# Layer 0's norm factor moved behind the projections: x transposed as it comes, norm weights applied as it leaves PSUM

## The chip, the cores and the metric

One core of a Trainium2 chip runs the whole program. The metric is the device time in microseconds of one execution. TensorE (PE) multiplies and transposes, VectorE (DVE), ScalarE (ACT) and GpSimd (POOL) work elementwise, SyncE (SP) issues most transfers. GpSimd has no part of PSUM in this kernel; VectorE and ScalarE empty it.

## What is computed

A two-layer encoder over 1024 tokens of width 1024. Layer 0 mixes by a neighbourhood attention with 16 heads, layer 1 by a grouped-query attention. The part that matters here is the head of layer 0:

```python
def rms_norm(x, g):
    xf = x.astype(jnp.float32)
    y = xf * lax.rsqrt(jnp.mean(xf * xf, axis=-1, keepdims=True) + NORM_EPS)
    return (y * g.astype(jnp.float32)).astype(x.dtype)

h = rms_norm(x, norm_g[0])
q, k, v, gate = jnp.split(h @ w_in, 4, axis=-1)     # w_in: 1024 x 4096
# attention of each query over an 8 x 16 window of the 16 x 64 grid, with a bias
x = x + (attention * silu(gate)) @ w_out
g = sigmoid(rms_norm(x, ple_norm_g[0]) @ ple_w_gate[0])
x = x + g * (p[0] @ ple_w_proj[0])
```

The norm factor of a token, r = rsqrt(mean(x^2) + eps), is one number per token; the norm weight norm_g[0] is one number per channel. A projection sums over channels, so r can be multiplied in after it.

## The kernel before

Tokens are kept in 8 tiles of 128. All products are made in float32r from a high and a low part: an operand is rounded (ScalarE writes the high part), the rest is found by subtraction (VectorE writes the low part), and three products high x high, high x low, low x high are summed in PSUM (`split3`, line 301 in the profile). The transposed input of the projections lies in `HTh` and `HTl` (channel on the partition, 8 token tiles x 8 channel blocks).

The program order is written out by hand: each engine runs its instructions in the order in which the Python code emits them. Two helpers shape that order. The class `Weights` (`WQ`) stages weight units of 128 x 1024 over SP's queue into `wstage`, and `pump` splits one into `wh` (ScalarE, line 216) and `wl` (VectorE, line 217; `settle` emits that half, at the next pump unless asked for earlier). `post` holds pieces of work that are emitted some steps later.

The opening of `mixer_a` (lines 695 to 780) makes the values V of heads 0 to 3 while x arrives. For each token tile: `square(t)` sums x^2 on ScalarE into `stat`; `newton(a, b)` finds r by small VectorE operations (lines 313 to 323, 714); `scale(t)` multiplies x by r and by the norm weights, which were broadcast to all partitions (`gain`, a transfer of 512 KB): for tiles 0, 1, 2, 4 and 6 in one VectorE operation (line 726), for 3, 5 and 7 on ScalarE (line 728) and then POOL (line 729). `ht(t)` transposes the eight 128 x 128 blocks on TensorE (line 426), rounds them out of PSUM (line 427) and subtracts (line 428). `vs[t][0]` and `vs[t][1]` are the two halves of the V projection of a tile, 12 products each; its eviction writes V's high part (ScalarE, line 580) and low part (VectorE, line 581). `weave` interleaves the Newton steps with other work. Transfers go out in the order x tile 0, gain, x tile 1, two weight units, x tiles 2 to 7, then the mask, the bias table and its rearrangement (`U`, `U2`).

After the opening, q and k of head 0 are projected (the first of those products has the form `d<-HTh,wh` of 128 x 512 on line 301), and then come 16 heads of attention, with the q/k projection of the next head, the gate projection and V of the next four heads as filling between the steps (`mix`). One step, for a head and a query tile: products S (`f_S`), bias and row minimum on VectorE (line 650, `sp` and `mn`), exponentials on ScalarE (line 659), transposes on TensorE (line 667), high and low parts `PTh` (ScalarE, line 670) and `PTl` (VectorE, line 671), products with V (`f_AV`). The eviction of a q/k projection (`qk_evac`) copies PSUM to `raw` (tile `th`) on ScalarE (line 594), then writes `QS`, `KA`, `KB` in three later pieces: two roundings on ScalarE (lines 597, 598), two differences and two copies on VectorE (601, 602, 603, 606). The eviction of a gate projection copies PSUM to `G` on ScalarE (line 521) and takes the tanh (line 522).

## Time and profile before

| what | us |
|---|---|
| three timed executions | 1574.35, 1575.03, 1576.03 |
| their median | 1575.03 |
| profiled execution, its time | 1577.5 |
| profiled execution, span from first to last instruction | 1575.6 |
| TensorE busy in the span | 1523.6 |
| VectorE busy | 1023.9 |
| ScalarE busy | 871.4 |
| POOL busy | 269.5 |

Busy times add up what each engine's instructions took; matmuls overlap, so TensorE's is not work at its peak. Around the span lie 1.9 us that no instruction shows. The mean granted TensorE clock is 0.997.

### The profile page before, as it was taken

The numbers are of one execution on the slowest core, as the hardware profiler recorded it, in microseconds if no ns is written. First come the engines' busy times: TensorE is split into PE (matmuls) and PEld (weight loads), VectorE is DVE, ScalarE is ACT, GpSimd is POOL, SyncE is SP. The second block draws the span as 40 slices with busy tenths as digits, with TensorE's granted clock in tenths as the row PEclk, the third lists the DMA queues.
The fourth block names the chain that finished last, engine by engine and source line by source line (L and its number), as shares of the span: only waits on it lengthen the run. The fifth ranks groups of instructions, "written<-read, shape, count | busy, mean of one in ns | idle before, by whom it ended". The sixth has DMA issues, their size and how long they took to land.

```text
span 1575.6 us, 24284 instructions
## 1 busy us (share of the span) xinstructions
PE 1523.6 (97%) x9048; PEld 1328.7 (84%) x9048; DVE 1023.9 (65%) x2062; ACT 871.4 (55%) x1744; POOL 269.5 (17%) x372
## 2 busy tenths in 40 slices
PE   6999999999999999999999999999999999999997
PEld 5888988988988788888988889989899888778886
DVE  6566576376467435648877786777777877525636
ACT  6465465366366622433467676766667767622422
POOL 2102102112022010000222132443131200000023
PEclk9999999999999999999999999999999999999999
DMA  8212122132122972142210111102111213651213
GB/s 272 78 45 65 53 80 78 39 92 78 39 79 77 343 257 68 54 140 94 74 49 21 38 51 41 58 24 65 39 32 43 74 41 112 223 201 54 71 55 129
DMA packets 89861, 138.84 MB, mean 88 GB/s; under 512 B 16912, under 2 KB 55952, under 8 KB 89744
## 3 DMA queue, kind: packets, MB, share of 16 engines
q1 hardware_dynamic: 85136, 122.62, 23.8%
q10 hardware_dynamic: 4608, 14.68, 2.6%
q8 instruction: 71, 1.16, 0.3%
q14 instruction: 46, 0.38, 0.1%
HBM read 104.65 MB, written 36.15 MB: 89 GB/s over the span
## 4 chain that ended last, share of the span: by engine, by line
PE 41%; DVE 7%; ACT 3%; issue 2%; ACTq 0%; DVEq 0%
PE d L301 21%; PE o L301 8%; PE t L1070 5%; PE s L301 5%; DVE PTl L1073 2%; DVE mn L1054 1%; ACT PTh L1072 1%; DVE wl L217 1%; PE t L426 1%; ACT wh L216 1%; PE t L1024 0%; ACT P L1060 0%; DVE QS L1034 0%; DVE ss L901 0%; DVE KB L965 0%
## 5 line engine op out<-in xcount | busy, mean ns | idle before, releaser
L301 PE MATMUL d<-wh,HTh 128*128 128x256 f32 (+1 forms) x1096 | 372.3, 340 | 5.0 <-ACT HTh L427 2.3
L301 PE MATMUL d<-wh,HTl 128*128 128x256 f32 (+1 forms) x1096 | 365.8, 334 | 1.5 <-DVE HTl L428 1.5
L301 PE MATMUL d<-wl,HTh 128*128 128x256 f32 (+1 forms) x1096 | 365.2, 333 | 0.0
L1073 DVE TENSOR_TENSOR PTl<-t,PTh 128x512 fp32r<-128x512 f32 x256 | 164.4, 683 | 114.8 <-ACT PTh L1072 114.4
L301 PEld LDWEIGHTS d<-wh,HTh 128*128 128x128 f32 x1096 | 207.7, 189 | 28.3 <-ACT HTh L427 2.9
L301 PEld LDWEIGHTS d<-wh,HTl 128*128 128x128 f32 x1096 | 207.7, 189 | 24.1 <-DVE HTl L428 2.2
L301 PEld LDWEIGHTS d<-wl,HTh 128*128 128x128 f32 x1096 | 208.0, 190 | 21.6
L301 PE MATMUL d<-HTh,wh 128*128 128x512 f32 x504 | 205.9, 409 | 0.0
L301 PE MATMUL d<-HTh,wl 128*128 128x512 f32 x504 | 197.8, 392 | 0.0
L301 PE MATMUL d<-HTl,wh 128*128 128x512 f32 x504 | 197.5, 392 | 0.0
L1060 ACT ACTIVATE P<-s,mn 128x1024 f32<-128x1024 f32 x128 | 142.7, 1114 | 66.6 <-DVE mn L1054 65.7
L301 PE MATMUL o<-PTl,V 128*128 128x256 f32 (+2 forms) x672 | 175.6, 292 | 3.3 <-DVE PTl L1073 2.2
L301 PE MATMUL o<-PTh,V 128*128 128x256 f32 (+2 forms) x672 | 174.2, 289 | 2.6 <-ACT P L1060 1.1
L1072 ACT ACTIVATE PTh<-t 128x512 fp32r<-128x512 f32 x256 | 139.4, 592 | 44.9 <-PE t L1070 44.3
L1054 DVE TENSOR_REDUCE mn<-s 128x1 f32<-128x1024 f32 x128 | 154.7, 1209 | 10.9 <-PE s L301 10.8
L1070 PE MATMUL t<-ident,P 128*128 128x128 f32 x1024 | 136.9, 275 | 7.6 <-DVE PTl L1073 6.1
L217 DVE TENSOR_TENSOR wl<-wstage,wh 128x1024 fp32r<-128x1024 f32 x89 | 113.8, 1284 | 40.8 <-ACT wh L216 40.3
L301 PEld LDWEIGHTS o<-PTl,V 128*128 128x128 f32 x672 | 128.9, 192 | 10.7 <-DVE PTl L1073 6.5
L301 PEld LDWEIGHTS o<-PTh,V 128*128 128x128 f32 x672 | 128.7, 192 | 8.3 <-issue 1.5
L1070 PEld LDWEIGHTS t<-ident,P 128*128 128x128 f32 x1024 | 115.0, 140 | 22.2 <-DVE PTl L1073 15.6
L301 PE MATMUL s<-KA,QS 128*128 128x512 f32 (+2 forms) x384 | 133.6, 402 | 0.0
L301 PE MATMUL s<-KB,QS 128*128 128x512 f32 (+2 forms) x384 | 121.8, 371 | 0.0
(178 smaller groups left out, 2436.9 us busy)
## 6 DMA issues: line engine op xcount, KB each, us to landing
wstage<-in_wts SPq DMA_DIRECT2D x92, 512.0 KB
X<-in_x SPq DMA_DIRECT2D x16, 512.0 KB
pp<-ppD SPq DMA_DIRECT2D x32, 256.0 KB
rb<-rD SPq DMA_DIRECT2D x56, 128.0 KB
ppD<-th SPq DMA_DIRECT2D x24, 256.0 KB
xD<-X SPq DMA_DIRECT2D x8, 512.0 KB
X<-xD SPq DMA_DIRECT2D x8, 512.0 KB
yD0h<-rb SPq DMA_DIRECT2D x14, 256.0 KB
```

What stands on the lines that cost most here:

```text
L216: act.activation(hi, s, AF.Copy)
L217: self.rest = lambda: dve.tensor_tensor(lo, s, hi, ALU.subtract)
L301: pe.matmul(ps, a, b, start=first, stop=last, skip_group_check=True)
L426: pe.transpose(ps[:, k], xn[:, (4 * c + k) * 128:(4 * c + k + 1) * 128], ident)
L1054: dve.tensor_reduce(mn, ps, axis=AX.X, op=ALU.min)
L1060: act.activation(p, ps, AF.Exp, bias=mn, scale=-1.0, accum_out=RS[h, hf][:, t:t + 1])
L1070: pe.transpose(ps[:, i], p[:, k * 128:(k + 1) * 128], ident)
L1072: act.activation(PTh[:, ks, c], ps, AF.Copy)
L1073: dve.tensor_tensor(PTl[:, ks, c], ps, PTh[:, ks, c], ALU.subtract)
```

## The change

The norm factor leaves the opening's path. x is transposed as it comes (`turn`); VectorE multiplies by the norm weights as the block leaves PSUM, where they are one number per partition and channel block (`gT`, a new input `gain0` of 128 x 8), into a float32 tile `xg`; ScalarE rounds `xg` to `HTh` (`high`), VectorE subtracts (`low`). So `HTh` and `HTl` hold x times the norm weights, without r, and r comes in where a projection leaves PSUM:

- V, where the token is the partition: the eviction scales by the column of `stat`. In the opening these evictions wait in the list `late` until r is known, and V's PSUM tiles alternate between two pools (`valloc`).
- q/k and gate, where the token runs along the free dimension: `spread_r` transposes broadcast columns of r on TensorE into `RB` (128 x 1024, every partition the same row), and `raw` and `G` are made by a VectorE product with `RB` instead of a ScalarE copy. In exchange one of the two copies in the eviction of q/k (line 603 before) goes from VectorE to ScalarE.

The gain broadcast, `scale`, and POOL's products with it are gone. x tile 0 comes in two halves, and the two weight units are issued ahead of x tile 1. Newton is done twice for four tiles, in the rounds t = 2 and t = 6. Ahead of and behind the transposes of tile 0 stand 12 and 10 transposes of the identity whose results nothing reads (`warm`, constants `WARM`).

```diff
+WARM = (12, 10)
...
+        "gain0": gains[0].reshape(8, 128).T,
...
-    def gate_items(key, pair, hf, alloc, sb, gg):
+    def gate_items(key, pair, hf, alloc, sb, gg, RB=None):
...
-            act.activation(G, ps, AF.Copy)
+            if RB is None:
+                act.activation(G, ps, AF.Copy)
+            else:
+                dve.tensor_tensor(G, ps, RB[:, hf * 512:(hf + 1) * 512], ALU.mult)
...
             def valloc():
+                early[1] += 1
+                if early[0] and early[1] % 2 == 0:
+                    return psO.tile([128, 512], F32, name="o")[:, :256]
                 return pd.tile([128, 512], F32, name="d")[:, :256]
...
-                    act.activation(V[:, t, :, 0:64], v, AF.Copy)
-                    dve.tensor_tensor(V[:, t, :, 64:128], v, V[:, t, :, 0:64], ALU.subtract)
+                    r = stat[:, 2, t:t + 1]
+
+                    def leave():
+                        act.activation(V[:, t, :, 0:64], v, AF.Copy, scale=r)
+                        dve.scalar_tensor_tensor(V[:, t, :, 64:128], v, r, V[:, t, :, 0:64], op0=ALU.mult, op1=ALU.subtract)
+                    if early[0]:
+                        late.append(leave)
+                    else:
+                        leave()
...
-                    act.activation(raw, ps, AF.Copy)
+                    dve.tensor_tensor(raw, ps, RB[:, s], ALU.mult)
...
-                        dve.tensor_copy(ka[lo, s], ka[hi, s])
+                        act.activation(ka[lo, s], ka[hi, s], AF.Copy)
...
-            def scale(t):
-                if t % 2 == 0 or t == 1:
-                    dve.scalar_tensor_tensor(X[t], X[t], stat[:, 2, t:t + 1], gt, op0=ALU.mult, op1=ALU.mult)
-                else:
-                    act.activation(X[t], X[t], AF.Copy, scale=stat[:, 2, t:t + 1])
-                    pool.tensor_tensor(X[t], X[t], gt, ALU.mult)
+            def turn(t, c):
+                ps = psT.tile([128, 4, 128], F32, name="t")
+                for k in range(4):
+                    pe.transpose(ps[:, k], X[t][:, (4 * c + k) * 128:(4 * c + k + 1) * 128], ident)
+                xg = ini.tile([128, 4, 128], F32, name="xg", bufs=4)
+                dve.tensor_tensor(xg, ps, gT[:, 4 * c:4 * c + 4, None].to_broadcast([128, 4, 128]), ALU.mult)
+                return lambda: high(t, c, xg), lambda: low(t, c, xg)
+
+            def high(t, c, xg):
+                act.activation(HTh[:, t, 4 * c:4 * c + 4], xg, AF.Copy)
+
+            def low(t, c, xg):
+                ks = slice(4 * c, 4 * c + 4)
+                dve.tensor_tensor(HTl[:, t, ks], xg, HTh[:, t, ks], ALU.subtract)
 
             def ht(t):
-                return [lambda c=c: to_ht(psT, t, X[t], (c,)) for c in range(2)]
-
-            load(0)
-            sync.dma_start(gt, bcast(gains, 0, D))
-            load(1)
+                (h0, l0), (h1, l1) = turn(t, 0), turn(t, 1)
+                h0()
+                l0()
+                h1()
+                l1()
+
+            def split():
+                WQ.pump(True)
+                WQ.settle()
+
+            def warm(n):
+                ps = psS.tile([128, 512], F32, name="s").rearrange("p (a c) -> p a c", a=4)
+                for k in range(n):
+                    pe.transpose(ps[:, k % 4], ident, ident)
+
+            def spread_r(hf):
+                ps = psT.tile([128, 4, 128], F32, name="t")
+                for t in range(4):
+                    i = 4 * hf + t
+                    pe.transpose(ps[:, t], stat[:, 2, i:i + 1].to_broadcast([128, 128]), ident)
+                act.activation(RB[:, hf * 512:(hf + 1) * 512], ps.rearrange("p t c -> p (t c)"), AF.Copy)
+
+            act.dma_start(gT, gain0)
+            for c in (slice(0, 512), slice(512, 1024)):
+                sync.dma_start(X[0][:, c], x[0][:, c])
             WQ.stage(True)
-            for t in range(2, NT):
+            for t in range(1, NT):
                 load(t)
...
+            act.activation(junk[:, :128], ident, AF.Square)
+            vs = [v_items(0, t) for t in range(NT)]
+            warm(WARM[0])
+            (h0, l0), (h1, l1) = turn(0, 0), turn(0, 1)
+            warm(WARM[1])
+            h0()
+            l0()
+            split()
+            h1()
+            l1()
+            split()
+            vs[0][0]()
+            ht(1)
+            vs[0][1]()
             square(0)
             square(1)
...
             for t in range(1, NT):
                 vs[t][0]()
                 if t + 1 < NT:
-                    weave(newton(4, 8) if t == 2 else [], ht(t + 1))
...
+                    square(t + 1)
+                    ht(t + 1)
+                if t in (2, 6):
+                    newton(t - 2, t + 2)
+                if t in (2, 3, 6, 7):
+                    late.pop(0)()
+                if t in (4, 7):
+                    spread_r(t // 6)
                 vs[t][1]()
+                if t in (2, 3, 6, 7):
+                    late.pop(0)()
```

More of the change, by code (lines that the diff above doesn't have):

```diff
@@ L566, in dalloc @@
                 return pd.tile([128, 512], F32, name="d")
+            early = [True, 0]
+            late = []
             def valloc():
+                early[1] += 1
+                if early[0] and early[1] % 2 == 0:
+                    return psO.tile([128, 512], F32, name="o")[:, :256]
                 return pd.tile([128, 512], F32, name="d")[:, :256]
@@ L696, in f_AV @@
                             later.add(FIN[0], fin)
+            stat = one.tile([128, 3, 8], F32, name="stat")
+            wk = one.tile([128, 24], F32, name="wki")
+            RB = one.tile([128, 1024], F32, name="RB")
             e2 = es.enter_context(ExitStack())
@@ L700, in mixer_a @@
             X = [ini.tile([128, D], F32, name=f"X{t}") for t in range(NT)]
-            gt = ini.tile([128, D], F32, name="gain")
+            gT = ini.tile([128, 8], F32, name="gT")
             junk = ini.tile([128, D], BF16, name="junk")
-            stat = one.tile([128, 3, 8], F32, name="stat")
-            wk = one.tile([128, 24], F32, name="wki")
             def load(t):
@@ L731, in ht @@
-            def ht(t):
-                return [lambda c=c: to_ht(psT, t, X[t], (c,)) for c in range(2)]
-            load(0)
-            sync.dma_start(gt, bcast(gains, 0, D))
-            load(1)
+                dve.tensor_scalar(ms, stat[:, 0, a:b], 1.0 / D, EPS, op0=ALU.mult, op1=ALU.add)
+                rsqrt(stat[:, 2, a:b], ms, wk)
+            def turn(t, c):
[5 more added lines that the diff above has]
+                return lambda: high(t, c, xg), lambda: low(t, c, xg)
@@ L741, in mixer_a @@
+            warm(WARM[0])
[10 more added lines that the diff above has]
+            vs[0][1]()
             square(0)
             square(1)
-            weave(newton(0, 1), [lambda: scale(0)])
-            WQ.pump(True)
-            WQ.pump(True)
-            vs = [v_items(0, t) for t in range(NT)]
-            weave(newton(1, 2), ht(0))
@@ L748, in mixer_a @@
-            scale(1)
-            square(2)
-            square(3)
-            vs[0][0]()
-            weave(newton(2, 4), ht(1))
-            scale(2)
-            scale(3)
-            square(4)
-            square(5)
-            square(6)
-            vs[0][1]()
             sync.dma_start(MK, mask)
@@ L764, in mixer_a @@
                 if t + 1 < NT:
-                    weave(newton(4, 8) if t == 2 else [], ht(t + 1))
-                if t == 1:
-                    square(7)
-                if t in (2, 3):
-                    scale(2 * t)
-                    scale(2 * t + 1)
+                    square(t + 1)
[6 more added lines that the diff above has]
+                    spread_r(t // 6)
                 vs[t][1]()
+                if t in (2, 3, 6, 7):
+                    late.pop(0)()
                 if t == 6:
@@ L779, in mixer_a @@
                         sync.dma_start(U2[:, r * 8:(r + 1) * 8, :], src)
+            post.flush()
+            early[0] = False
             e2.close()
```

18 lines of the change are left out of this document (5 added, 13 removed).

## The prediction

> **What bounds the kernel now.** I read the page first, then the opening stage by stage, then who keeps TensorE waiting there.
>
> ```profile
> span 1575.6 us, 24284 instructions
> ...
> PE 1523.6 (97%) x9048; PEld 1328.7 (84%) x9048; DVE 1023.9 (65%) x2062; ACT 871.4 (55%) x1744; POOL 269.5 (17%) x372
> ```
>
> The page's busy times: TensorE is the bound of the whole, so a saving counts only where TensorE stands still. The next two fences are the table by stages (window, its length, busy time and instruction count of PE, PEld, DVE, ACT, POOL, then clock, DMA share, GB/s) and the waits of TensorE in the first 75 us (total, times, longest).
>
> ```profile
> 32.00:40.00 8.00, 6.72 (x58) 6.51 (x57) 6.95 (x8) 5.76 (x9) 5.03 (x2) 1.00 0.60 183
> ...
> 200.00:400.00 200.00, 197.10 (x1129) 172.32 (x1128) 128.88 (x295) 118.03 (x265) 35.33 (x48) 1.00 0.23 70
> ```
>
> ```profile
> PE t L426 <- DVE X L726: 11.6, 4, 8.8
> PE d L301 <- ACT HTh L427: 2.3, 2, 1.2
> PE d L301 <- DVE HTl L428: 1.5, 2, 1.3
> ```
>
> In layer 0's attention TensorE works 197.1 of 200 us. In the opening it does not: 15.4 us of waits, 11.6 of them for the normalised x (8.8 before its first instruction), 3.8 for the rounded halves, with VectorE busy 6.95 of 8 us in the window shown. The change works exactly there. The timeline gives the opening's steps (start, duration, engine, line).
>
> ```profile
> 0.99 0.29 POOL masks.py:199 TENSOR_SCALAR_AFFINE_SELECT ident<-ident 128x128 f32<-128x128 f32 x1
> 4.19 1.06 ACT L710 ACTIVATE junk<-X 128x1024 bf16<-128x1024 f32 x1 [2.19 <-DMA X<-in_x]
> 8.78 1.94 PE L426 MATMUL t<-ident,X 128*128 128x128 f32 x8 [8.78 <-DVE X L726]
> 9.06 1.06 ACT L216 ACTIVATE wh<-wstage 128x1024 fp32r<-128x1024 f32 x1
> 10.15 1.22 DVE L217 TENSOR_TENSOR wl<-wstage,wh 128x1024 fp32r<-128x1024 f32 x1 [1.52 <-ACT wh L216]
> 10.33 1.06 ACT L216 ACTIVATE wh<-wstage 128x1024 fp32r<-128x1024 f32 x1 [0.21 <-DMA wstage<-in_wts]
> 11.93 0.58 PE L301 MATMUL d<-wh,HTh 128*128 128x256 f32 x1 [1.21 <-ACT HTh L427]
> ...
> 14.66 0.41 PE L301 MATMUL d<-wl,HTh 128*128 128x256 f32 x1
> 14.88 0.41 PE L301 MATMUL d<-wh,HTl 128*128 128x256 f32 x1
> ```
>
> x tile 0 has landed at 4.19; square, Newton steps, scaling, transposes and rounding pass before the first product at 11.93. Products then start 0.22 apart; later, below, 0.12 apart: TensorE begins at half clock.
>
> ```profile
> 12.25 1.06 ACT L710 ACTIVATE junk<-X 128x1024 bf16<-128x1024 f32 x1
> 13.43 1.06 ACT L710 ACTIVATE junk<-X 128x1024 bf16<-128x1024 f32 x1
> 26.81 1.03 PE L426 MATMUL t<-ident,X 128*128 128x128 f32 x8
> 26.92 0.16 DVE L714 TENSOR_SCALAR stat<-stat 128x4 f32<-128x4 f32 x1
> 29.12 0.28 PE L301 MATMUL d<-wh,HTh 128*128 128x256 f32 x1
> 29.24 0.28 PE L301 MATMUL d<-wl,HTh 128*128 128x256 f32 x1
> 29.66 0.16 DVE L323 SCALAR_TENSOR_TENSOR stat<-wki 128x4 f32<-128x4 f32 x1
> 49.74 0.40 PE L301 MATMUL d<-HTh,wh 128*128 128x512 f32 x1
> ```
>
> The last row is the end of the stage: the first product of the q/k projection, at 49.74. That is the mark I move.
>
> **The change, part by part.** Prices not yet shown, from the groups of instructions (the number after the bar is busy time, the next the mean in ns): a VectorE product of a PSUM tile into f32 (L1204, as xg, raw and G will be), a ScalarE rounding from SBUF (L509), and the two V evictions.
>
> ```profile
> L1204 DVE TENSOR_TENSOR X<-d,X 128x512 f32<-128x512 f32 x16 | 11.0, 689 | 26.6 <-PE d L301 14.7 <-DMA X<-in_x 11.9
> L509 ACT ACTIVATE rb<-Y 128x512 fp32r<-128x512 f32 x10 | 6.2, 622 | 12.5 <-POOL Y L513 12.5
> L580 ACT ACTIVATE V<-d 128x256 fp32r<-128x256 f32 x8 | 3.0, 379 | 4.8 <-PE d L301 4.8
> L581 DVE TENSOR_TENSOR V<-d,V 128x256 fp32r<-128x256 f32 x7 | 2.9, 419 | 4.4 <-ACT V L580 4.4
> ```
>
> So xg costs 0.65 started back to back, a rounding (h) 0.6, the low part (l) 0.65, a weight split 1.06 on ScalarE then 1.22 on VectorE, a square 1.18 (12.25 to 13.43), Newton for four tiles 2.3 (26.92 to 29.82 less one 0.6 eviction inside), eight transposes 1.94 or 1.03, a product 0.22 or 0.12.
>
> First product. ident is ready at 1.28. Twelve stand-in transposes at 0.24 end at 4.2, when x has landed. Tile 0's two halves leave TensorE at 5.15 and 6.1, ten more stand-ins end by 8.5. VectorE in its order: xg0 5.2 to 5.85, xg1 6.1 to 6.8, l0 6.8 to 7.5, wl0, l1, wl1. ScalarE: h0 5.9 to 6.5, wh0 6.5 to 7.5, h1 to 8.1, wh1 to 9.15. Hence wl0 7.55 to 8.8, l1 to 9.5, wl1 to 10.7. TensorE needs wl0 for its second product: it runs on from 8.8, not 11.93 to 12.9. Both weight units are issued after x tile 0 now, with the gain broadcast gone and x tile 1 behind them. They were the fourth and fifth transfer and had landed by 9.06 and 10.33; as the second and third I take them as landed in time (7.5 and 8.1 are needed); the bound is that they land as before, a rival below. The split of x into two transfers costs SP one more issue, gT costs ScalarE's queue one, ahead of its first work; both are covered by the wait until 4.19.
>
> The run of tiles, with the clock at half until about 12. Eleven products at 0.21 end at 11.1, tile 1's transposes at 12.6, vs[0] at 14.05. xg 12.1 to 13.45, h to 14.1, l0 to 14.1, l1 to 14.8; vs[1][0] ends at 15.35. Tile 2: transposed by 16.4, but three squares (1.18 each) stand ahead of its h on ScalarE: h0 17.65 to 18.2, l0 to 18.85, vs[2][0] ends 20.05. Tile 3: l0 at 22.55, vs[3][0] ends 24.0. Now the first added wait: Newton holds VectorE 23.2 to 25.5, V0 and V1 follow (ScalarE, then VectorE, to 26.7), and behind them are queued tile 4's xg on VectorE and a square and h on ScalarE. So l0 of tile 4 is at 28.65; TensorE stands still for 2.1 us; vs[4][0] ends 29.85. Tiles 5, 6, 7 then go at TensorE's pace (four VectorE operations of 0.65 lie inside its 1.03 + 24 x 0.12): vs[5][0] 34.05, vs[6][0] 38.05, vs[7][0] 41.85. The second added wait: the spread of r for tiles 4 to 7 is queued on TensorE ahead of vs[7][1] and needs the second Newton (41.3 to 43.6): 1.75 us of standstill, 0.5 of transposes, then 1.45 of products. The q/k projection begins at 45.55: 4.2 us gained. Had the clock stayed up from 8.8, vs[0][0] would end at 10.1, and with wl1 (10.7) binding, vs[1][0] at 13.85, everything 1.5 us earlier: 44.05, 5.7 us gained.
>
> Which clock? The clock's own windows show in the trace: it drops twice, each time for 3.41 us. First three rows: busy time of line 301's products alone in such a window; next three: all engines in the window right after each; the last by itself: all engines in the first of the windows.
>
> ```profile
> 1343.29:1346.70 3.41, 1.12 (x6) 0.62 (x5) 1.00 0.96 344
> 1370.60:1374.01 3.41, 0.48 (x2) 0.28 (x2) 1.00 0.24 91
> 1565.16:1568.57 3.41, 1.17 (x10) 0.96 (x9) 1.00 0.00 0
> ```
>
> ```profile
> 1346.70:1350.11 3.41, 3.41 (x24) 2.97 (x23) 1.91 (x3) 0.77 (x3) 0.00 (x0) 1.00 0.90 252
> 1374.01:1377.42 3.41, 3.41 (x16) 3.41 (x17) 0.96 (x3) 0.00 (x0) 0.00 (x0) 0.50 0.00 0
> 1568.57:1571.98 3.41, 0.00 (x0) 0.00 (x0) 2.41 (x11) 1.23 (x3) 0.00 (x0) 0.50 0.37 154
> ```
>
> ```profile
> 1343.29:1346.70 3.41, 2.40 (x18) 1.94 (x17) 3.31 (x7) 2.54 (x5) 0.00 (x0) 1.00 0.96 344
> ```
>
> A window with 1.17 us of products lost the clock, one with 1.12 us kept it; the one that kept it held twelve transposes besides (18 instructions, 6 of them products; 2.40 us in all). So transposes seem to count, and the stand-ins can raise the clock. But once raised, by about 5.3, they run twice as fast, end near 6.6, and TensorE idles until 8.8: a window with about 1.4 us of work, nearer to the 1.17 that lost the clock than to the 2.40 that kept it. If the window's edge falls two microseconds later, the clock holds. The edge is free, so I take the middle of the two ends: 5.0 us gained in the opening.
> The Trainium skill ("TensorE: Matmul & The Clock Gate", Part 4) states that transposes do not count as TensorE activity for the clock; the first and third of these rows speak against it. By the rule alone the sum would be the half-clock one, 4.2 us.
>
> Layer 0's attention. 32 raw evictions and 16 gate evictions move from ScalarE to VectorE, 32 copies of ka the other way.
>
> ```profile
> L594 ACT ACTIVATE th<-d 128x512 f32<-128x512 f32 x25 | 14.9, 595 | 17.1 <-PE d L301 16.8
> L598 ACT ACTIVATE KA<-th 64x512 fp32r<-64x512 f32 x25 | 15.7, 629 | 0.5
> L603 DVE CAST KA<-KA 64x512 fp32r<-64x512 f32 x25 | 11.2, 447 | 0.8
> L659 ACT ACTIVATE sp<-sp,mn 128x384 f32<-128x384 f32 x73 | 44.8, 613 | 5.3 <-DVE mn L650 4.7
> ```
>
> ```profile
> PE t L667 <- ACT sp L659: 5.3, 7, 1.5
> ```
>
> VectorE: 48 x 0.69 - 32 x 0.45 = +18.7 us, from 64% to about 69% of the stage. ScalarE: -48 x 0.595 + 32 x 0.63 = -8.4 us. The moved eviction waits for the end of its product group on VectorE as it did on ScalarE (0.67 us each, 16.8 over 25). Queued behind it are row minima and PTl, whose own products come later on TensorE anyway, and deferred splits, which have time; TensorE waits for those only through the exponentials, 5.3 us in 370, and these waited 4.7 us for minima. Bounds: all of these waits go (-5.3), or every added VectorE microsecond arrives (+18.7). I take +0.5, near the lower end, because so little waits on VectorE now and ScalarE is relieved at once. POOL loses its three products with the gain, which nothing waits for any more. V's low part as a scalar-tensor-tensor costs like L581.
>
> Sum: -5.0 + 0.5 = -4.5 us. The span would be 1571.1; the profiled execution took 1577.5, so 1573.0 for its like. The median of the timed runs, 1575.03, lies 2.5 below the profiled time: 1570.5 on that scale.
>
> **The rivals.** The clock comes late: stand-ins do nothing, and the half-clock sum holds. 1575.03 - 4.2 + 0.5 = 1571.3. (The rule of the Trainium skill named above would lead here.) For it: eight transposes at 8.78 did not raise the clock; against it: they filled only half a window.
> The opening's cover fails: the weights land no earlier than before, wh0 starts at 9.06 and wh1 at 10.33 as now. wl0 then ends at 11.35 (9.06 + 1.06 + 1.22) instead of 8.8, 2.5 us later, and the gain halves: 1573.0. For it: all transfers are in flight together, so two places in the order may bring little; against it: the 512 KB of gain are gone.
> VectorE becomes the bound in the attention: in heads without a V projection a raw eviction lands ahead of a row minimum, the exponential, the transposes and PTl slip with it. If half of the 18.7 us arrives: 1575.03 - 5.0 + 9.4 = 1579.4, slower. It decides from 44% of 18.7 on (8.2 us); against it: 4.7 us of waits for minima in the whole stage.
>
> **How the numbers follow.** A measurement of this kernel can tell 0.2%, 3.15 us: faster is below 1571.9, slower above 1578.2. Forecast 0.46, late clock 0.20, late weights 0.20, VectorE bound 0.14. The forecast's own spread (opening 4.2 to 5.7 gained, attention -2 to +2) reaches 1567.3 to 1572.8, nearly all of it faster; three quarters of the late clock is faster, a fifth of the late weights; the rest of these is the same; the last case is slower. That gives 0.63 faster, 0.23 same, 0.14 slower. The range goes from 1566.5 (clock up throughout and some exponentials no longer waiting) to 1577.0 (late weights with a few microseconds of the attention's price) and leaves most of the last case outside.
>
> **What would show it.** Right: first product with a weight near 8, running on before 9; first q/k product between 44 and 45.6; TensorE waits of 1.5 to 2.5 us near tile 4, and one before the spread of tiles 4 to 7 that ends with Newton; no POOL product in the opening; TensorE's waits for exponentials in layer 0 still 4 to 8 us. Wrong: weights landing at 9 or later; products 0.21 apart long after 12; waits for exponentials or PTl above 10 us; or a difference that arises after the first layer.

## The result and the profile after

The changed kernel takes 1582.23 us (median of five runs, 1579.52 to 1588.88), the kernel before 1575.63 beside it (1574.35 to 1577.30): ratio 1.0048, 95% interval 1.0029 to 1.0068. It is slower by some 7 us, where I had forecast 4.5 faster. The profiled execution took 1582.23, its span is below.

The page's head: every engine has about the work that it had. TensorE's 30 instructions more are the 22 stand-ins and the eight transposes of r; nothing here explains 7 us.

```profile
span 1580.4 us, 24374 instructions
...
PE 1530.3 (97%) x9078; PEld 1333.5 (84%) x9078; DVE 1041.6 (66%) x2069; ACT 866.4 (55%) x1728; POOL 261.7 (17%) x369
```

The opening, from TensorE's timeline (start, duration, engine, line):

```profile
5.67 1.60 PE L765 MATMUL s<-ident 128*128 128x128 f32 x10
7.41 0.38 PE L303 MATMUL d<-wh,HTh 128*128 128x256 f32 x1
8.67 0.38 PE L303 MATMUL d<-wl,HTh 128*128 128x256 f32 x1 [0.88 <-DVE wl L219]
8.89 0.28 PE L303 MATMUL d<-wh,HTl 128*128 128x256 f32 x1
...
47.33 0.40 PE L303 MATMUL d<-HTh,wh 128*128 128x512 f32 x1
```

Products run from 8.67 us, 0.12 apart soon after, as the forecast had it with the clock up. But the first q/k product stands at 47.33: 2.4 us ahead of 49.74, not 5.0. TensorE's waits in the first 75 us (total, times, longest) name the places:

```profile
PE t L771 <- DVE stat L325: 2.6, 1, 2.6
PE d L303 <- ACT HTh L745: 1.8, 1, 1.8
...
PE t L771 <- DVE xg L741: 1.1, 1, 1.1
```

The lead of 2.4 us is then lost in layer 0's attention. Put the same transposes of both traces side by side: at head 0 the changed kernel is 2.4 us ahead, when the dense phase after layer 0's attention begins it is 5.4 behind, and until 1200 us nothing changes any more. At each of heads 4, 8 and 12 it loses some 1.25 us (at head 4 from 0.7 ahead to 0.6 behind: the transposes that started at 198.62 start at 199.21), at head 2 1.2 us, and twice some 1.5 us in a window of 3.41 us at half clock. The windows before those two, and one of the two (window, its length, then busy time and instructions of PE, PEld, DVE, ACT, POOL, clock, DMA share, GB/s):

```profile
374.99:378.40 3.41, 1.33 (x8) 1.15 (x9) 2.32 (x5) 2.55 (x5) 3.25 (x3) 1.00 0.38 118
378.40:381.82 3.42, 3.42 (x13) 2.93 (x12) 2.67 (x6) 3.00 (x6) 0.00 (x0) 0.50 0.44 136
545.65:549.07 3.42, 1.46 (x7) 0.84 (x5) 0.87 (x2) 2.08 (x4) 0.00 (x0) 1.00 1.03 413
```

Before lost the clock twice as well, at 1374 us and, with no TensorE work left, at 1569, both outside the stretch that is compared.

What happens at head 4 is seen on ScalarE's timeline. First the kernel before, then the changed one, then VectorE of the changed one:

```profile
193.13 0.59 ACT L594 ACTIVATE th<-d 128x512 f32<-128x512 f32 x1
...
194.58 0.62 ACT L597 ACTIVATE QS<-th 64x512 fp32r<-64x512 f32 x1
195.23 0.63 ACT L598 ACTIVATE KA<-th 64x512 fp32r<-64x512 f32 x1
195.88 0.49 ACT L670 ACTIVATE PTh<-t 128x384 fp32r<-128x384 f32 x1
197.07 0.62 ACT L659 ACTIVATE sp<-sp,mn 128x384 f32<-128x384 f32 x1 [0.70 <-DVE mn L650]
```

```profile
196.11 0.63 ACT L615 ACTIVATE QS<-th 64x512 fp32r<-64x512 f32 x1 [2.50 <-DVE th L612]
196.76 0.63 ACT L616 ACTIVATE KA<-th 64x512 fp32r<-64x512 f32 x1
197.42 0.63 ACT L621 ACTIVATE KA<-KA 64x512 fp32r<-64x512 f32 x1
197.96 0.47 ACT L688 ACTIVATE PTh<-t 128x384 fp32r<-128x384 f32 x1
198.45 0.61 ACT L677 ACTIVATE sp<-sp,mn 128x384 f32<-128x384 f32 x1
```

```profile
192.01 3.46 DVE L219 TENSOR_TENSOR wl<-wstage,wh 128x1024 fp32r<-128x1024 f32 x2
195.40 0.68 DVE L612 TENSOR_TENSOR th<-d,RB 128x512 f32<-128x512 f32 x1
```

Before, ScalarE made raw itself (`th`, 193.13) and could round QS and ka at once. Now raw comes from VectorE, where it stands behind two weight low parts (3.46 us). ScalarE, which works in its order, waits 2.50 us at the rounding of QS, and the rounding PTh and the exponential that TensorE needs are queued behind it, with one copy more in front of them. TensorE stands still at two places where it ran on before:

```profile
196.60 0.45 PE L303 MATMUL o<-PTl,V 128*128 128x384 f32 x1 [0.45 <-DVE PTl L689]
199.21 0.55 PE L685 MATMUL t<-ident,sp 128*128 128x128 f32 x3 [0.79 <-ACT sp L677]
```

The first wait is VectorE's order: raw (0.68 us) now stands between the weight low parts and PTl. The second is ScalarE's: the row minimum was done at 197.11, but the exponential began at 198.45, behind QS, KA, the ka copy and PTh. Heads 8 and 12 show the same pair (0.43 and 0.79, 0.44 and 0.78). Over the stretch from 65 to 545 us the groups of instructions (busy time, mean ns, then idle time before them and its releaser) show this wait as new; first before, then after:

```profile
L597 ACT ACTIVATE QS<-th 64x512 fp32r<-64x512 f32 x30 | 18.6, 621 | 0.1
L522 ACT ACTIVATE th<-G 128x512 f32<-128x512 f32 x16 | 10.1, 632 | 0.5
```

```profile
L615 ACT ACTIVATE QS<-th 64x512 fp32r<-64x512 f32 x30 | 18.7, 624 | 14.6 <-DVE th L612 14.6
L527 ACT ACTIVATE th<-G 128x512 f32<-128x512 f32 x16 | 10.1, 632 | 22.0 <-DVE G L526 22.0
```

### The profile page after: what moved, and what is told of

Its sections match the earlier page's. It is cut to its first block, busy times and chain, and to the rows that moved or that the text cites. A ratio compares the mean times of both kernels' runs of the same rounds, so it can differ in the third digit from the quotient of the medians.

```text
span 1580.4 us, 24374 instructions
## 1 busy us (share of the span) xinstructions
PE 1530.3 (97%) x9078; PEld 1333.5 (84%) x9078; DVE 1041.6 (66%) x2069; ACT 866.4 (55%) x1728; POOL 261.7 (17%) x369
## 4 chain that ended last, share of the span: by engine, by line
PE 40%; DVE 7%; ACT 3%; issue 2%; DMA 0%; ACTq 0%; SPq 0%; POOL 0%; DVEq 0%; POOLq 0%
PE d L303 21%; PE o L303 8%; PE t L1114 5%; PE s L303 5%; DVE PTl L1117 2%; DVE mn L1098 1%; ACT PTh L1116 1%; PE t L428 1%; DVE wl L219 1%; PE t L1068 1%; ACT P L1104 1%; ACT wh L218 0%; DVE QS L1078 0%; DVE Y L444 0%; ACT th L527 0%
## 5 line engine op out<-in xcount | busy, mean ns | idle before, releaser
L303 PE MATMUL d<-wh,HTh 128*128 128x256 f32 (+1 forms) x1064 | 363.3, 341 | 6.0 <-ACT G L549 2.2
L303 PE MATMUL d<-wh,HTl 128*128 128x256 f32 (+1 forms) x1064 | 356.6, 335 | 0.5 <-DVE HTl L749 0.4
L303 PE MATMUL d<-wl,HTh 128*128 128x256 f32 (+1 forms) x1064 | 356.1, 335 | 0.9 <-DVE wl L219 0.9
L303 PEld LDWEIGHTS d<-wh,HTh 128*128 128x128 f32 x1064 | 201.4, 189 | 29.6 <-ACT G L549 2.6
L303 PEld LDWEIGHTS d<-wl,HTh 128*128 128x128 f32 x1064 | 201.7, 190 | 22.6 <-DVE wl L219 1.1
L303 PEld LDWEIGHTS d<-wh,HTl 128*128 128x128 f32 x1064 | 201.3, 189 | 23.0 <-DVE HTl L749 1.1
```

The lines of the kernel that those rows point to most:

```text
L303: pe.matmul(ps, a, b, start=first, stop=last, skip_group_check=True)
```

## The experiments

### Which part loses

Times are medians; the difference is to the kernel before on the same chip. The edits are shown abridged. The runs of the opening alone leave r out of q, k and the gate.

**The opening alone.** The changed kernel with, in the attention, the old lines:

```
-dve.tensor_tensor(raw, ps, RB[:, s], ALU.mult)
+act.activation(raw, ps, AF.Copy)          # G likewise, ka copy back on dve
```

> The changed opening alone: raw and G leave PSUM by ScalarE's copy as before, and the copy to ka's low half is VectorE's again; factor r is thereby left out of q, k and the gate of layer 0. Theory (VectorE's evictions in layer 0's attention cost what the opening gains, and more): the opening's 2.4 us stay, about 1573 us, faster than before by 1 to 3 us, and heads 4, 8 and 12 lose nothing at step 4 (1.3 us each in the change). Rival (the attention loses because it starts earlier against its DMAs and GpSimd's chain, whoever evicts): 1577 us or more, slower than before, with the lead of 2.4 us gone by head 3. Second rival (half-clock windows alone made the difference): within 1 us of the change's own time less 1.6 us for each window that is not there.

1576.60, ratio 1.0014 (1.0004 to 1.0024). No gain: the theory's 1573 fell, though heads 4, 8 and 12 lose nothing here, as it said. The trace shows why, below.

**The attention alone.** The kernel before with `RB` set to ones and the three edits:

```
+pool.memset(RB, 1.0)
-act.activation(raw, ps, AF.Copy)
+dve.tensor_tensor(raw, ps, RB[:, s], ALU.mult)      # G likewise
-dve.tensor_copy(ka[lo, s], ka[hi, s])
+act.activation(ka[lo, s], ka[hi, s], AF.Copy)
```

> The kernel before with the attention's part alone: raw and G of layer 0 are VectorE products with a tile of ones in the place of r, and the copy to ka's low half is ScalarE's. Theory: about +1.3 us at each of heads 4, 8 and 12, some more at one or two other places, in sum +4 to +8 us, 1580 to 1584 us. Rival (the change's loss comes from the earlier start, not from who evicts): within 1 us of the kernel before. My prediction's term was +0.5 us.

1580.78, ratio 1.0043 (1.0031 to 1.0055): 6.0 us slower, at full clock throughout the stretch. 1.0014 times 1.0043 is 1.0057, within the interval of the whole change. So the attention's edits are the loss, and the opening is no gain.

### Why the attention loses

**The ka copy back on VectorE**, in the changed kernel:

```
-act.activation(ka[lo, s], ka[hi, s], AF.Copy)
+dve.tensor_copy(ka[lo, s], ka[hi, s])
```

> The change with the copy to ka's low half back on VectorE (31 copies, 0.63 us each on ScalarE). Theory (at heads 4, 8 and 12 two things add: raw waits behind two weight low parts on VectorE, and ScalarE's three late copies then stand in front of an exponential): ScalarE has one copy less there, 0.5 us gained at each of the three heads, 1580 to 1581.5 us. Rival (VectorE is the one that is full): 1 to 4 us slower than the change, since VectorE gets 31 copies more. Second rival: no difference beyond 1 us, the copy is beside the path.

1581.93, ratio 1.0041 (1.0027 to 1.0056): no difference from the change. In the trace the waits of 0.79 us for an exponential at the three heads fall to 0.27, as the theory said. But the wait of 0.45 us for PTl stays, and later in each of these heads a wait of some 0.25 us for an exponential is new: the heads lose about as much as in the change.

**raw alone** (G and the ka copy as before):

> The kernel before with one of the attention's three edits: raw leaves PSUM as a VectorE product with a tile of ones; G and the copy to ka's low half stay where they were. The trace of the attention's edits alone shows TensorE losing 1.07 us at each of heads 4, 8 and 12 (0.79 of it for an exponential behind ScalarE's three late copies, the rest for PTl), 1.25 at head 2 and 0.79 at head 6. Theory (raw behind two weight low parts on VectorE, then the ScalarE copies late): without ScalarE's ka copy the wait for sp at heads 4, 8 and 12 goes, 0.4 us each stays; +1 to +3 us, 1576 to 1578 us. Rival (the raw eviction is the whole of it, the other two edits nothing): 1580 to 1581 us. Second rival (G's eviction is the costly one): within 0.5 us of before.

1580.41, ratio 1.0032 (1.0021 to 1.0043): the whole loss, within the intervals. G's eviction costs nothing that shows, although it makes ScalarE's tanh wait 22 us.

**raw multiplied later.** ScalarE copies raw out of PSUM as before, VectorE multiplies it one item later, G and ka on VectorE:

```
 act.activation(raw, ps, AF.Copy)
+post.add(1, lambda: dve.tensor_tensor(raw, raw, RB[:, s], ALU.mult))
```

> The kernel before with raw copied from PSUM by ScalarE as there, and multiplied by the tile of ones on VectorE one step later, from SBUF to SBUF; G is a VectorE product, the copy to ka's low half is VectorE's. Theory (it matters that the eviction stands behind weight low parts, not how much VectorE has to do): nothing at heads 4, 8 and 12, -1 to +1.5 us against before, 1574 to 1576.5 us. Rival (VectorE's added work is the loss: it now has 31 products and 31 copies more than in the change's attention has room for): 1580 us or more.

1588.63, ratio 1.0086 (1.0069 to 1.0103). My theory, that the eviction's place behind the weight low parts is what counts, fell; the rival, VectorE's added work, looked right.

**Copies by DMA, and r on GpSimd**, each in the kernel before, tell VectorE's time from raw's maker:

```
-dve.tensor_copy(kb[lo, s], kb[hi, s])      # ka likewise
+sync.dma_start(kb[lo, s], kb[hi, s])       # raw and G are VectorE products
```

> The attention's edits in the kernel before (raw and G as VectorE products with a tile of ones), but the copies to the low halves of ka and kb, two for each half of a head, by DMA instead of on an engine (head 0 keeps them on VectorE). In the windows 65 to 545 us VectorE is busy 296 us before, 309 with the change's attention, 325 with raw multiplied later; the loss is 0, 6 and 14 us. Theory (what counts is VectorE's added time; some third to half of it reaches TensorE): VectorE falls to about 296 again, and the loss goes: 1573 to 1576 us. Rival (what counts is when raw is evicted, at heads 4, 8 and 12 behind two weight low parts): the steps of 0.9 us there stay, 1576.5 to 1579 us. Second rival (the copies land late): new waits of TensorE for ka or kb, 1580 us or more.

```
+post.add(1, lambda: pool.tensor_tensor(raw, raw, RB[:, s], ALU.mult))   # G likewise; splits at 4, 6, 8
```

> The kernel before with raw and G copied by ScalarE as there, and multiplied by the tile of ones on GpSimd (46 products of 128x512, 1.4 to 1.6 us each by the rows of Y, 70 us on an engine that is busy 77 of 480), tanh and the splits some steps later. Theory (VectorE's added time is the loss): 0 to +3 us against before, the rest because VectorE's instructions run longer beside GpSimd's; 1574 to 1577 us. Rival (VectorE loses as much beside GpSimd as it would by doing the products): 1579 us or more. Second rival (the later splits make a new wait for QS or KB): waits of TensorE's s for QS in the trace, over 1580 us.

1578.77 (1.0024, 1.0014 to 1.0035) and 1594.41 (1.0123, 1.0109 to 1.0137). The stage table, 65 to 545 us, fifth and sixth number the busy time and instructions of VectorE: the kernel before, copies by DMA, r on GpSimd.

```profile
65.00:545.00 480.00, 471.38 (x2693) 410.70 (x2691) 295.68 (x669) 279.88 (x624) 77.03 (x103) 1.00 0.27 85
```

```profile
65.00:545.00 480.00, 472.12 (x2693) 410.83 (x2691) 296.27 (x654) 254.89 (x578) 75.91 (x103) 1.00 0.33 101
```

```profile
65.00:545.00 480.00, 460.90 (x2604) 402.48 (x2604) 295.81 (x657) 269.13 (x602) 140.01 (x149) 0.98 0.23 70
```

VectorE (295.7, 296.3, 295.8 us) is as busy as before in both, and they lose 3.6 and 19.2 us. So the sum of VectorE's time is not the cause either. What goes with the loss is ScalarE's wait at the rounding of QS; its row in the waits of ScalarE (same stretch) with copies by DMA, in the attention alone, in raw alone, with raw later, with r on GpSimd:

```profile
ACT QS L600 <- DVE th L597: 13.4, 9, 2.4
```

```profile
ACT QS L600 <- DVE th L597: 14.4, 9, 2.4
```

```profile
ACT QS L597 <- DVE th L594: 16.9, 12, 2.4
```

```profile
ACT QS L603 <- DVE th L600: 25.7, 19, 2.5
```

```profile
ACT QS L609 <- POOL th L606: 28.7, 14, 7.0
```

0.1 us before goes with a loss of nothing, then 13.4, 14.4, 16.9, 25.7 and 28.7 us with 3.6, 6.0, 6.4, 14.6 and 19.2. The order is the same in these five, but the sum of these waits is no price: the change itself (14.6 us) and e3 (17.1) lose the same, and 6.0 and 6.4 us can't be told apart. r on GpSimd loses besides by three stretches at half clock. The traces of raw alone and of copies by DMA are of executions below their medians (1578.29 and 1576.85); the second falls only 0.6 us behind before by the end of the attention. So that ScalarE's wait is on the path is seen at heads 4, 8 and 12; how much of the loss is its own, and how much VectorE's order ahead of PTl, these runs do not divide.

**raw held back** where it stands behind the two low parts (three halves of heads), with the splits of these halves two items later, in the whole change with the best opening and copies by DMA, which is the kernel to compare it with:

```
+if h % 4 == 1 and h > 1 and hf == 0:       # ScalarE copies, product three items later
+    act.activation(raw, ps, AF.Copy); post.add(3, lambda: dve.tensor_tensor(raw, raw, RB[:, s], ALU.mult))
```

> The whole change, r included, with the opening of the run before and the ka and kb copies by DMA from head 1 on. Theory: the sum of that opening (-2 to -3.5 us) and of the attention with copies by DMA (+1.4 us in its trace, +3.6 in the medians): 1572.5 to 1576.5 us, within 0.1% of before, and 6 to 9 us faster than the change. Rival (starting earlier, the attention loses more to GpSimd's chain): 1577 us or more.

> The run before, but the one raw of heads 4, 8 and 12 that stands behind two weight low parts (3.46 us on VectorE) is copied by ScalarE and multiplied three items later, behind PTl and the row minimum. Theory (there it is the place in VectorE's queue): the steps of 0.44 for PTl and 0.44 for the exponential go at the three heads, 1.5 to 2.5 us faster than the run before. Rival (it is VectorE's time there as elsewhere): no difference beyond 1 us, as the product is only moved by about 1 us.

1576.77 (1.0017, 1.0008 to 1.0026) without and 1582.66 (1.0050, 1.0038 to 1.0062) with it. The first, with r in its place, starts the attention 4.1 us ahead of before and loses it there, and is still 5 us faster than the change. The second fell out as neither theory had it: three products, moved behind PTl and the row minimum, cost 6 us. ScalarE's row at head 4 shows most of it: with PTh and the exponential behind it, QS now waits

```profile
194.28 0.63 ACT L624 ACTIVATE QS<-th 64x512 fp32r<-64x512 f32 x1 [3.04 <-DVE th L619]
```

and the three heads lose 2.1 us each by the starts of the same transposes, where the run without the hold lost 0.8: 3.9 of the 6 us. The waits for PTl at these heads are gone, so here ScalarE's wait acts alone: the row minimum was done at 193.65, the exponential began at 196.09, and TensorE waited 1.51 us for it. What was not tried is to take the wait away: r on VectorE with the rounding of QS and ka issued late enough that it never waits.

### Where the opening's gain goes

**Without the stand-ins** (`WARM` left out of the change):

> The change without its 22 stand-in transposes. The trace of the change shows the clock at full from 6.35 us, before the first product. Theory (the stand-ins brought the clock up): the first products run at 0.24 us apart until a window with enough of them has passed, some 3 to 6 us of the opening at half speed; first q/k product 1 to 2.5 us later (48.3 to 49.8), total 1583 to 1585 us. Rival (transposes of the stand-in do nothing for the clock, or the weights set the pace): first q/k product within 0.4 us of 47.3 and the total within 1 us of the change.

1588.01, ratio 1.0079 (1.0067 to 1.0091): some 5 us slower than the change and 6 slower than the run of e3. The products stand 0.21 apart until 14.9 us, and the first q/k product is at 51.50. The stand-ins do raise the clock.

But 22 of them don't hold it in every execution. In the profile of the opening alone (e1) the window after the clock came up, then the two that follow:

```profile
5.67:9.08 3.41, 1.64 (x12) 1.20 (x11) 1.78 (x4) 2.14 (x4) 0.00 (x0) 1.00 1.00 393
9.08:12.50 3.42, 2.56 (x12) 2.56 (x13) 2.54 (x3) 1.02 (x2) 0.00 (x0) 0.50 1.02 418
12.50:15.91 3.41, 3.41 (x18) 3.41 (x17) 2.10 (x4) 1.41 (x3) 0.00 (x0) 0.50 1.03 417
```

With 1.64 us of work in it the clock falls to half for two windows, and the first q/k product is at 50.38, behind 49.74. What leaves this window so empty is the weight: ScalarE begins to round it at 7.58 us, after 1.17 us of waiting for its transfer, and TensorE waits 1.76 us for it ahead of the first product (8.68). In the changed kernel's own profile the rounding began at 6.32, the window of 6.36 to 9.77 us held 2.38 us, and the clock stayed. That profile had luck: of the eleven with this opening, nine began the rounding between 7.17 and 7.81, and only e15 (6.25) as early. In e3 too the first q/k product is at 50.41.

**More stand-ins, later spreads** (opening alone):

```
-WARM = (12, 10)
+WARM = (12, 30)          # and warm(10) ahead of tiles 4 and 5
-if t in (4, 7): spread_r(t // 6)
+if t == 5: spread_r(0)   # spread_r(1) inside head 0's q/k projection
```

> The opening alone (as in the first run: no factor r in q, k and gate) with 20 more stand-in transposes before the first product, 10 more before the products of tiles 4 and 5, and the two spreads of r later: behind tile 5's and inside the first q/k projection. Theory (the clock is lost between 6 and 9.4 us and between 26 and 30 us because TensorE is busy less than about 1.9 of 3.4 us there: 1.31, 1.55, 1.60 and 1.64 us lost it in the traces, 1.90 and 2.38 kept it): no half-clock window in the opening, first q/k product at 45 to 46.5 us, 1571.5 to 1573.5 us, and the runs closer together than the 1574.5 to 1583.3 of the first. Rival (transposes of this kind do not hold the clock): first q/k product at 49.5 or later and 1576 us or more. Second rival (what is gained at the start is given back in the attention's early heads to DMA waits): first q/k product early, but 1574.5 us or more.

```profile
6.65:10.06 3.41, 3.14 (x29) 2.94 (x27) 1.91 (x3) 2.46 (x3) 0.00 (x0) 1.00 1.02 410
...
44.20:47.61 3.41, 1.42 (x12) 1.22 (x11) 2.59 (x12) 0.90 (x3) 1.08 (x3) 1.00 0.00 0
```

```profile
47.76 0.80 PE L303 MATMUL d<-HTh,wh 128*128 128x512 f32 x1 [2.14 <-DVE V L592]
```

1576.26, ratio 1.0012 (1.0001 to 1.0023). The clock holds from 6.65 us, but the wait for r at the end comes back in another form: the q/k projection needs a buffer of PSUM that V's eviction frees, and this one waits for the second Newton. The stall then drops the clock at 47.61. With the late product on top (whole change, ka on VectorE) it was

> The whole change, its factor r included, with the filled opening of the run before, with raw copied by ScalarE and multiplied by r on VectorE one step later, and with the ka copy on VectorE. Theory: the sum of the two runs before: 1571.5 to 1574 us, faster than the kernel before by 1 to 3 us. Rival (VectorE is full): 1577 us or more.

1588.35, ratio 1.0083 (1.0068 to 1.0098), as raw later alone.

**Newton earlier**, split into tiles 4 to 6 and 7:

> The filled opening, with the second Newton for tiles 4 to 6 moved ahead of tile 6's transposes and one of its own for tile 7 (again without r in q, k and gate). The trace of the filled opening shows the products of tile 7 ended by 45.4 us and the first q/k product at 47.76, behind V's eviction of tile 4, which waited for the second Newton (43.19 to 46.7 us). Theory (r's last link sets the end of the opening, the clock is its second price): the wait of 2.1 us falls below 0.5, first q/k product at 45.3 to 46 us, no half-clock window there, 1570.5 to 1572.5 us. Rival (the opening's lead is given back at heads 2, 6, 10 and 14, where TensorE waits for an exponential behind GpSimd's chain and a DMA): lead at head 1 but 1573.5 us or more.

```profile
PE t L768 <- DVE xg L738: 2.6, 1, 2.6
```

1576.37, ratio 1.0009 (1.0000 to 1.0017). A third form of the same wait: Newton waits for a square ahead of tile 6's xg on VectorE, and TensorE for that xg.

**q/k of head 0 in the s buffers**, which nothing of the opening holds:

```
-proj_T(("aqk", h), hf, dalloc, ...)
+proj_T(("aqk", h), hf, dalloc if h else salloc, ...)
```

> The filled opening alone (without r in q, k and gate), with head 0's two q/k halves in the s buffers of PSUM in place of the d buffers, so that they wait for no eviction of V and so for no Newton. Theory (the wait for r at the opening's end and the lost clock are the two prices): the wait of 2.1 us at 47.8 goes, first q/k product at 45.4 to 46 us, no half-clock window in the opening, first exponential 2.5 to 4 us ahead of before; 1571 to 1573 us. Rival (the lead is given back at heads 2, 6, 10 and 14): the same start, but over 1574 us. Second rival (again another wait takes its place, as with the early Newton): first exponential less than 1.5 us ahead.

The first q/k product is at 45.34 us, 4.4 ahead, at full clock; so 4.4 of the forecast's 5.0 for the opening were to be had. By the first exponential of each head the trace leads by 3.9 us at head 0, by 2.9 at the least on the way and by 4.0 at head 15: the attention, with ScalarE's evictions, keeps most of it. Yet the kernel takes 1575.61, ratio 1.0002 (0.9993 to 1.0011). The lead falls to 0.9 us at the end of layer 0's attention. The rows of waits there, first before, then this run, and the windows at that place:

```profile
ACT th L544 <- DMA ppD<-th: 1.1, 1, 1.1
PE o L301 <- ACT PTh L670: 1.0, 1, 1.0
```

```profile
PE o L303 <- ACT PTh L688: 2.2, 1, 2.2
ACT th L546 <- DMA ppD<-th: 1.8, 1, 1.8
```

```profile
535.46:538.87 3.41, 1.02 (x5) 0.77 (x6) 1.62 (x4) 1.46 (x3) 0.00 (x0) 1.00 1.04 410
538.87:542.28 3.41, 3.41 (x12) 2.73 (x12) 0.42 (x1) 1.62 (x3) 0.00 (x0) 0.50 1.01 397
```

ScalarE waits there for a store to DRAM to free `th`. Who comes earlier waits longer (2.2 us for 1.0), and the longer wait drops the clock: together some 3 us. That is one profiled execution; that the store sets this time in all of them is not shown.

**Stand-ins in the kernel before** (50 from the start, 12 ahead of the first product):

> The kernel before with 50 stand-in transposes from the start and 12 ahead of the first product, nothing else. In the trace of before the first products stand 0.24 us apart, and 0.12 only from 15.7 us. Theory (the clock alone is worth something in either opening): products 0.12 apart from the first on, at 11.9 us; 1 to 2 us gained if the weights and tiles keep up, 1572 to 1573.5 us. Rival (tiles and scales set the pace there): within 0.5 us of before.

1576.26, ratio 1.0008 (1.0000 to 1.0017). Products 0.12 apart from 13.25 us, and the q/k projection at 50.02: there the tiles set the pace, and the clock alone is worth nothing.

### Versions that might beat both

**Copies by DMA in the kernel before:**

> The kernel before with the ka and kb copies by DMA from head 1 on, 27 us of VectorE's work in layer 0's attention taken away and nothing else. Theory (VectorE has room there before: 296 of 480 us, TensorE waits only 7 us for exponentials): -1.5 to +0.5 us. Rival (VectorE's time is paid at a third or more even there): 1.5 us or more faster, up to 9. Second rival (the DMAs delay the others): slower by over 1 us.

1573.97, ratio 0.9994 (0.9985 to 1.0002): not to be told from before, with 24 us less on VectorE.

**Y split later.** ScalarE also stands some 4 us at `rb<-Y` for GpSimd's Y at heads 2, 6 and 10, in both kernels. `YS = (11, 11)` to `(20, 11)`, in the improved change (e14) and in the kernel with copies by DMA (e16):

> The whole change with the filled opening, head 0's q/k in the s buffers and the copies by DMA (1576.8 us), and ScalarE's split of Y nine items later in layer 0 (YS 20 in place of 11). The traces show ScalarE at heads 2, 6, 10 and 14 standing 4 to 5 us at rb<-Y for GpSimd's Y, with PTh and an exponential queued behind it, TensorE waiting 0.7 to 2.1 us for each, and half-clock windows behind the longer of these waits (127 and 376 us). Theory (the opening's lead is lost there, in the attention's VectorE evictions and at the end of layer 0's attention): those four waits and their windows go, 4 to 6 us gained, 1571 to 1573 us, faster than the kernel before. Rival (the stall moves: GpSimd's Y is later as well, or the split meets another exponential): within 1.5 us of 1576.8.

> The kernel before with the copies by DMA (1574.0 us) and the same later split of Y. It shows what the change is worth when neither version has these waits. Theory: four waits of 0.8 to 1.5 us go, 3 to 5 us gained, 1569 to 1571.5 us, so that the improved change is still 1 to 3 us slower than the improved kernel before (the attention's edits cost more than the opening saves). Rival (the opening's 4 us of lead now arrive at the end): the improved change is faster by 1 us or more.

1582.08 (1.0038, 1.0024 to 1.0051) and 1586.37 (1.0061, 1.0049 to 1.0074): 5.9 and 10.2 us slower than before, the rival's case. The stall moves to a buffer of Y that a store has not left (e18, head 2):

```profile
136.54 0.59 ACT L478 ACTIVATE Y<-o 64x512 f32<-64x512 f32 x1 [4.23 <-DMA yD0l<-Y]
```

Here the improved change is the faster of the two, by 4.3 us; as both are slower than before, I take nothing from that but that the order can turn. No version ran measurably faster than the kernel before.

## Why the prediction was wrong, step by step

**The attention's term is the step that failed**: +0.5 us was taken, the edits alone measured +6.0. The sentence that failed is that the deferred splits behind the moved eviction "have time". They had time on VectorE. But the first of them, the rounding of QS and ka, is ScalarE's, and was free of waits only because ScalarE had made raw itself. Moving raw to VectorE put a wait for another engine into ScalarE's order, ahead of PTh and of the exponentials. I named what queues behind raw on VectorE, and not who waits for raw. A second sentence failed too, that the products of the queued PTl "come later on TensorE anyway": at heads 4, 8 and 12 TensorE waits 0.44 us for PTl behind raw, and 0.79 for the exponential. That raw's move costs the 6 us is shown by raw alone (+6.4); how these divide between the two orders stays open.

**The bound was read from the wrong row.** I took the value near the lower end because TensorE waits for the exponentials through minima only (4.7 us). The total rose from 5.3 before to 8.6 in the changed kernel

```profile
PE t L685 <- ACT sp L677: 8.6, 9, 2.1
```

in 375 us, just above the 4 to 8 that I had called right. That rise of 3.3 us is less than half of the 7.8 us between 2.4 ahead and 5.4 behind. The sums of waits miss what the starts of the same instruction in both traces show, and the clock that is lost after a wait.

**The rival "VectorE becomes the bound" had the sign and a part of the mechanism.** It gave 1579.4 from half of 18.7 us arriving. VectorE rose by 12.5 us in the stretch (295.7 to 308.2), but kernels with no rise lost 3.6 and 19.2 us. It was right that PTl slips behind raw on VectorE; the exponential slipped with its minimum already done, by ScalarE's order.

**The opening's term was 5.0 and measured 2.4 in the change's profile, nothing in the median of the opening alone.** Right were: the first product near 8 (7.41, running on from 8.67); no GpSimd product with the norm weights (those of the attention's table run from 42.97 us); the wait at tile 4 (2.1 worked out, 1.8 measured); a wait before the spread of tiles 4 to 7 that ends with Newton. With the clock up, as it was in that profile, I had 44.05 for the first q/k product; it came at 47.33. Of these 3.3 us, 0.9 is a term mis-sized (the wait for the second spread, 2.6 and not 1.75, as Newton took 3.5 us and not 2.3), 1.1 is a wait missed before the first spread (a weight low part fell ahead of tile 5's xg); the rest lies over the tiles and isn't placed. The rival of late weights fell in this profile and in e15's, and came in part in the others. My own schedule has the first weight rounded from 6.5 on, so it is needed then and not by 7.5; nine of the eleven profiles had it between 7.17 and 7.81, late by 0.7 to 1.3 us, short of the rival's 9.06. e13 shows that 4.4 was to be had once nothing at the end waited for r.

**The clock.** That the clock could be held or lost in the opening is what the runs show: held with 2.38 us in the window of the changed kernel's profile, lost with 1.64 in e1's. But I looked to the window's edge alone (6.36 and 5.67 us there), and the weight differed more. I priced the loss at 1.5 us. In e1 the first q/k product is 3.1 us later than in the change's profile (50.38 for 47.33); 1.3 of these stand at the first product already, for the weight, and some 1.8 are left for the clock. What I had not priced is that each later stall of TensorE can cost another window.

## What to carry over

When an operation moves to another engine, list the readers of its result: each that stays behind gains a wait between engines, and on an engine that works in order everything queued after that reader can gain it too. List also what stands behind the operation in its new engine's order. A saved microsecond ahead of a fixed landing, here in e13's profile a store that frees a buffer, becomes a longer wait, and a wait of some 2 us can cost a window of half clock besides. Compare the starts of the same instruction in two traces, since the sums of TensorE's waits showed less than half of the loss here.

## What was not expected of the hardware

Stand-in transposes raise the clock: it came up at 6.36 us in the changed kernel, after nothing but stand-ins and eight transposes of x, against 14.9 us without the stand-ins. With 20 more of them the window of 6.65 to 10.06 us in e7 held 3.14 us of work, and the clock stayed. The Trainium skill ("TensorE: Matmul & The Clock Gate", Part 4) says of a transpose in TensorE's transpose mode that the full clock doesn't engage for it, as it doesn't count as busy in the same way. The transposes of these runs, which the profile lists as MATMUL, do raise the clock; whether they run in that mode the profile doesn't show.

The clock falls without an idle window. The Trainium skill (the same page, Part 1) lets it fall after a window of some 3.4 us that is idle. Here windows of 3.41 us with 1.02, 1.33, 1.42, 1.46 and 1.64 us of work each were followed by one at half clock, and 2.38 and 3.14 were not. In between, the busy time alone doesn't decide: 1.50 us in e8 (from 377.49) and 1.55 in e1 (from 46.63) kept the clock, 1.89 in the kernel before (from 1370.60) lost it.

Small VectorE operations slowed down beside GpSimd. Newton's steps on 128x4 elements, before and during GpSimd's table:

```profile
42.82 0.16 DVE L325 SCALAR_TENSOR_TENSOR wki<-wki 128x4 f32<-128x4 f32 x1
42.97 2.10 POOL L643 TENSOR_TENSOR tb<-MK,u 128x128 f32<-128x128 f32 x5 [41.69 <-DMA u<-U]
...
43.89 0.38 DVE L325 SCALAR_TENSOR_TENSOR wki<-wki 128x4 f32<-128x4 f32 x1
```

Five of them took 0.38 to 0.42 us, and the path that ended the opening grew by 1.1 us in all.
